# A two-layer hybrid attention encoder on one core: latent norms and latent outputs at other places in the order, part of the far shares on ScalarE, gains first in SP's queue

## The chip, the cores and the metric

The kernel runs on one core of one Trainium2 chip. Its engines are TensorE (PE, with PEld for the loading of weights), VectorE (DVE), ScalarE (ACT), GpSimd (POOL) and SyncE (SP, which here only issues transfers). The metric is the time of one execution on the device in microseconds (us); less is better.

## The reference

The input x is 512 positions by 1024 channels, float32. Two layers, each `x = x + concat(a, b) @ w_out`, and a last RMS norm. In a layer:

```
h = rms_norm(x, norm_g);  p = h @ w_in
c_q (384), c_kv (256), k_r (32), gate_a (512), dil_qkv (3 x 3 x 512), gate_b (512) = split(p)
a = mla_attention(c_q, c_kv, k_r) * silu(gate_a)
b = dilated_attention(dil_qkv) * silu(gate_b)
```

`mla_attention` norms the two latents c_q and c_kv (an RMS norm each), multiplies them up to queries, keys and values of 8 heads (64 plain and 32 rotary dimensions; one rotary key for all heads), and attends over all positions. `dilated_attention` has three groups of 8 heads of 64, with windows (128, 1), (512, 4) and (2048, 16) of (width, dilation), that is banded attention among neighbours and among every fourth and every sixteenth position; the outputs of the three groups are added with weights, the softmax over the groups' log-sums of exponentials, per position and head.

## The kernel before, in words

**Arithmetic.** Activations lie transposed, channels on partitions, in 8 tiles `h` of 128 x 512. Every operand of a large product is split into a high and a low part (`split`, L220: a cast on ScalarE, L221, and a subtraction on VectorE, L222), and a product is three matmuls (`triple`, L239: L241, L242, L243) of 512 columns. Weights come tile by tile from memory through SP's queue (`prefetch`, L189: L195), three tiles ahead of their use; ScalarE casts them (L198), and the low part is made by VectorE (L203) or, for most projections, by a negation on ScalarE (L200) and an accumulating load on GpSimd's queue (L201). A half chunk, that is 4 tiles of h against one weight tile, is 12 matmuls.

**The order.** All instructions are emitted by one planner, `Weave` (L76). It has a main line, TensorE's long products in the order of `forward_order` (L29), and side lines: `nline` (norms), `sline` (scores), `tline` (transposes of P and the products with V), `cline` (the combination of groups and the gated outputs). Each task is a generator that emits some instructions and yields an estimate of TensorE's time and a pause; the planner's clock is the sum of these estimates. A task has needs, (other task, lag): it may start when the clock has passed the end of the other by the lag. After each step of the main line the side lines are looked at, one task at a time in each; a line's next task waits for the one before it. When the main line is blocked, side steps are forced without regard to lags. What is emitted is then scheduled into the engines' queues by the framework, in which an instruction whose buffer isn't free can fall behind later ones. The planner's us are near TensorE's, but not the same.

**The parts that the change touches.**
- The start (L286 to L310): ScalarE's queue issues the first weight tile, the 26 columns of gains (`gn`, L289) and the second weight tile; SP's queue issues the 8 tiles of x (L298) and the other weight tiles. WARM matmuls on a zero tile (L296) run before the data are there. `take_x` (L270) multiplies x by the gains of the norm (L273, L274); the first products are L376.
- The latent norm (`latent_norm`, L388), task `lcq`: the squares of the query latent, added by GpSimd (L354), are transposed by TensorE (L256) and summed, 1/rms is worked out on VectorE in some 12 small instructions, and after a pause LN it is spread over partitions by TensorE (L236). `mla_rope`, task ("mur", 0), needs its end.
- The latent outputs (`mla_out`, L556, task "mo", one for each pair of heads): gate times output (`gated`, L430: L433), split into hl (L221, L222). They stand in `cline` between the combinations (`combine`, "do1", L813, and `combine_last`, "do", L835), in the order of the tasks that they belong to; the fourth "mo" comes after "do1" of pair 2. The output projection needs all four: `out_part` in layer 0, `out_rows` (L882) in layer 1.
- The far units (units 2 to 5 and 8 to 11: groups 1 and 2). `far_scores` (L727) makes scores, exponentials (L757) and, for group 2 in its second part, the groups' shares (`shares`, L795: L804 on ScalarE, L810 on VectorE the last), with which the 8 blocks of P are multiplied on GpSimd (L765). `far_out` (L768) transposes P (L449), splits it, and multiplies it with V in four steps (L785), each merged by ScalarE (L788) and VectorE (L789, L791). The lag between scores and transposes is LG2 = 16.5 for group 2 (units 4, 5, 10, 11) and LG = 6.0 for the others.

Of the kernel before, what the change touches and what calls it, by code (L numbers as in the profile page):

```python
# [11 lines left out]
ALU = mybir.AluOpType  # L12
# [10 lines left out]
AHEAD, RATE, LAG, CAP = 3, 451.1, 2.5, 34.9  # L23
STEP, LD0, WARM, LG2, LY = 2, 10.0, 11, 16.5, 5.0
LV = 3.0
LG, LP, LD, LM, LC, LN, LX, LF = 6.0, 0.25, 8.25, 2.0, 14.25, 5.75, 5.0, 0.25
SHUF = [i + 8 if i < 8 else i - 8 if i < 16 else i for i in range(32)]

def forward_order():  # L29
    return [('ckv',), ('v', 1, 0), ('cq', 2), ('cq', 0), ('cq', 1), ('dqk', 0, 0), ('dqk', 0, 1), ('nv', 0), ('mur', 0), ('ga', 0), ('dqk', 1, 0), ('kr',), ('dqk', 1, 1), ('nv', 1), ('muq', 0), ('muk', 0), ('mv', 0), ('muq', 1), ('dqk', 2, 1), ('muk', 1), ('dqk', 2, 0), ('muq', 2), ('dqk', 3, 1), ('muq', 3), ('dqk', 3, 0), ('dqk', 4, 1), ('mur', 1), ('v', 2, 0), ('muq', 4), ('dqk', 4, 0), ('dqk', 5, 0), ('muk', 2), ('ga', 1), ('muq', 5), ('dqk', 5, 1), ('mv', 1), ('dqk', 6, 0), ('nv', 2), ('gb', 0), ('muq', 6), ('dqk', 6, 1), ('muq', 7), ('nv', 3), ('dqk', 8, 0), ('gb', 1), ('muk', 3), ('v', 1, 1), ('ga', 2), ('dqk', 7, 0), ('dqk', 7, 1), ('dqk', 10, 0), ('dqk', 8, 1), ('dqk', 9, 0), ('dqk', 9, 1), ('v', 2, 1), ('dqk', 10, 1), ('ga', 3), ('dqk', 11, 0), ('dqk', 11, 1), ('gb', 2), ('gb', 3)]  # L30


def unit(u):

    return u % 6 // 2, 2 * (u // 6) + u % 2
# [102 lines left out]
def hybrid_encoder(ctx, tc, xT, wst, gains, fgain, tables, keytab, masks, out):  # L138
    nc = tc.nc
# [35 lines left out]
    gn = const.tile([128, 2 * NG], F32, name="gn")  # L175
# [102 lines left out]
    for l in range(DEPTH):  # L278
        L = Layer()
# [7 lines left out]
    load_w = lambda q, k: q.dma_start(raws[k], wst[k, :, 0:384])  # L287
    load_w(nc.scalar, 0)
    nc.scalar.dma_start(gn, gains)  # L289
    load_w(nc.scalar, 1)  # L290
    nc.scalar.activation(ones[:, 1:2], ones[:, 0:1], AF.Exp)
# [435 lines left out]
    def far_scores(L, u, part):  # L727
# [3 lines left out]
        g, p = unit(u)  # L731
# [3 lines left out]
        pt = t([128, S], F32, "p", 8)  # L735
# [3 lines left out]
        for j in range(2):  # L739
            b = 2 * part + j  # L740
# [19 lines left out]
        if g == 2 and part:  # L760
            shares(L, p)
            for b in range(4):
                for a in range(2):
                    pt = L.p["d", u, b // 2][:, 256 * (b % 2) + 128 * a:256 * (b % 2) + 128 * a + 128]
                    nc.gpsimd.tensor_scalar(pt, pt, L.share[p][:, b, 2, a:a + 1], 0.0, op0=ALU.mult, op1=ALU.add)  # L765
        yield 0.44, 0.5
# [164 lines left out]

    main, nline, sline, tline, cline = ([] for _ in range(5))
    for L in layers:
# [7 lines left out]
        task(nline, k("lckv"), later(k("ckv"), k("norm")), latent_norm, "ckv")  # L941
        task(nline, k("lcq"), later(*[k("cq", c) for c in range(3)], k("norm")), latent_norm, "cq")
        for o in ORDER:
# [43 lines left out]
        for _, (what, n), needs, scores, f in sorted(att, key=lambda x: x[0]):  # L987
            if scores:
                task(sline, k("s0", what, n), [(x, LM if what == "m" else LD0 if n == 0 else LD) for x in needs], scores, n, 0)
                task(sline, k("s", what, n), now(*before[0]), scores, n, 1)  # L990
                task(tline, k("o", what, n), [(k("s", what, n), LG2 if what == "d" and unit(n)[0] == 2 else LG)], f, n)
                before = [before[1], [("t", l, what, n)]]
            else:
                task(cline, k(what, n), needs, f, n)
        mla = [k("mo", p) for p in range(4)]
# [30 lines left out]

    Weave(RATE, CAP).run(main, [nline, sline, tline, cline])

# [114 lines left out]
```

## Time and profile before

| what | us |
|---|---|
| median of 3 runs | 930.44 (928.4 to 932.7) |
| the profiled execution, its own time | 929.99 |
| its span, first to last instruction | 928.2 |
| TensorE busy | 908.0 |
| VectorE, ScalarE, GpSimd busy | 692.4, 597.6, 313.2 |

In a row of the timeline stand start, duration, engine, line, operation, out<-in by the program's names, sizes, a count, and in brackets the idle time of the engine before it with what ended it. A "q" behind an engine's name is its sequencer, which issues transfers. Matmuls overlap, so their durations are longer than their spacing. The first products of layer 1 begin near 463 us.

### The profile page before, as it was taken

The page shows a single profiled execution, that of the slowest core. Times are in us where ns is not written, and L with a number is a line of the kernel's source. Part 1 is how long each engine was busy: PE and PEld are TensorE (multiplying, and loading weights), DVE is VectorE, ACT ScalarE, POOL GpSimd, SP SyncE. Part 2 cuts the span into 40 slices and gives each one's busy share as a digit, 9 for nine tenths or more (in the row PEclk, how much of TensorE's full clock was granted, in tenths as well). Part 3 has the DMA queues.
Part 4 walks back from the last instruction along what each step waited for, and adds up shares of the span by engine and source line. Part 5 has one row for each costly group of instructions (what it writes and reads, how often), then busy time and mean ns, then how long its engine had stood idle before and what let it go on. Part 6 is the DMA issues. An engine that isn't in the chain of part 4 may idle for free.

```text
span 928.2 us, 15855 instructions
## 1 busy us (share of the span) xinstructions
PE 908.0 (98%) x5175; PEld 773.4 (83%) x5175; DVE 692.4 (75%) x1733; ACT 597.6 (64%) x1449; POOL 313.2 (34%) x365
## 2 busy tenths in 40 slices
PE   9999999999999999999999999999999999999996
PEld 7978888988889889887897888889888888898785
DVE  6756787877868776688766679787878676767964
ACT  6546876667757766764445468756768586676533
POOL 0134253345542432233211343524464234224300
PEclk9999999999999999999999999999999999999998
DMA  8457453276554764664453653615667558367542
GB/s 271 121 124 146 97 123 69 65 163 148 122 124 93 148 125 107 137 155 132 166 169 95 146 121 82 126 40 134 138 126 158 129 101 167 78 142 138 147 125 91
DMA packets 86466, 118.14 MB, mean 127 GB/s; under 512 B 16944, under 2 KB 37232, under 8 KB 86384
## 3 DMA queue, kind: packets, MB, share of 16 engines
q1 hardware_dynamic: 66656, 81.59, 30.6%
q0 software_dynamic: 19296, 35.14, 24.0%
q8 instruction: 41, 0.67, 0.3%
q10 hardware_dynamic: 432, 0.41, 0.1%
q14 instruction: 41, 0.34, 0.1%
HBM read 112.74 MB, written 4.36 MB: 126 GB/s over the span
## 4 chain that ended last, share of the span: by engine, by line
PE 83%; DVE 8%; ACT 4%; issue 2%; DMA 1%; POOL 1%; ACTq 0%; DVEq 0%; POOLq 0%
PE bank L241 22%; PE bank L242 22%; PE bank L243 22%; PE bank L449 5%; PE bank L550 3%; PE bank L376 3%; PE bank L744 1%; PE bank L785 1%; PE bank L673 1%; DVE pt L222 1%; DVE whl L203 1%; ACT whl L198 1%; DMA p<-wst 1%; DMA wraw<-wst 1%; DVE tmp L630 1%
## 5 line engine op out<-in xcount | busy, mean ns | idle before, releaser
L241 PE MATMUL bank<-hl,whl 128*128 128x512 f32 x712 | 283.9, 399 | 2.2 <-ACT hl L221 1.3
L242 PE MATMUL bank<-hl,whl 128*128 128x512 f32 x712 | 278.3, 391 | 0.0
L243 PE MATMUL bank<-hl,whl 128*128 128x512 f32 x712 | 278.1, 391 | 0.0
L198 ACT CAST whl<-wraw 128x512 fp32r<-128x512 f32 (+3 forms) x243 | 143.8, 596 | 121.2 <-PE bank L243 80.2
L201 POOL DMA_DIRECT2D whl<-wst x134 | 117.9, 884 | 225.2 <-ACT whl L200 152.7
L243 PEld LDWEIGHTS bank<-hl,whl 128*128 128x128 f32 x712 | 133.6, 188 | 29.5 <-DMA whl<-wst 0.4
L241 PEld LDWEIGHTS bank<-hl,whl 128*128 128x128 f32 x712 | 133.7, 188 | 28.5 <-ACT hl L221 1.7
L242 PEld LDWEIGHTS bank<-hl,whl 128*128 128x128 f32 x712 | 134.0, 188 | 23.9 <-DVE hl L222 0.3
L241 PE MATMUL bank<-whl,hl 128*128 128x256 f32 (+2 forms) x328 | 99.6, 304 | 1.6 <-ACT hl L221 1.6
L243 PE MATMUL bank<-whl,hl 128*128 128x256 f32 (+2 forms) x328 | 97.9, 298 | 0.0
L242 PE MATMUL bank<-whl,hl 128*128 128x256 f32 (+2 forms) x328 | 97.7, 298 | 0.0
L628 POOL TENSOR_TENSOR tmp<-tmp,sd 128x512 f32<-128x512 f32 x48 | 63.2, 1316 | 91.9 <-DVE tmp L626 65.4
L203 DVE TENSOR_TENSOR whl<-wraw,whl 128x512 fp32r<-128x512 f32 (+3 forms) x109 | 76.6, 710 | 23.1 <-ACT whl L198 22.1
L222 DVE TENSOR_TENSOR pt<-bank,pt 128x512 fp32r<-128x512 f32 x128 | 83.6, 684 | 5.4 <-ACT pt L221 4.0
L200 ACT ACTIVATE whl<-wraw 128x512 fp32r<-128x512 f32 x134 | 85.0, 634 | 0.1
L221 ACT CAST pt<-bank 128x512 fp32r<-128x512 f32 x128 | 69.9, 588 | 10.7 <-PE bank L449 10.3
L530 POOL TENSOR_SCALAR p<-p,lc 128x512 f32<-128x512 f32 x64 | 48.8, 769 | 70.0 <-DVE lc L529 64.2
L449 PE MATMUL bank<-ident,p 128*128 128x128 f32 x512 | 67.7, 275 | 0.0
L241 PEld LDWEIGHTS bank<-whl,hl 128*128 128x128 f32 x328 | 62.3, 190 | 3.9 <-ACT hl L221 1.8
L243 PEld LDWEIGHTS bank<-whl,hl 128*128 128x128 f32 x328 | 62.3, 190 | 2.0 <-DVE hl L222 0.4
L242 PEld LDWEIGHTS bank<-whl,hl 128*128 128x128 f32 x328 | 62.4, 190 | 1.7
L449 PEld LDWEIGHTS bank<-ident,p 128*128 128x128 f32 x512 | 59.2, 142 | 5.4
(181 smaller groups left out, 1620.1 us busy)
## 6 DMA issues: line engine op xcount, KB each, us to landing
wraw<-wst SPq DMA_DIRECT2D x218, 256.0 KB, 3.1
whl<-wst POOLq DMA_DIRECT2D x134, 256.0 KB, 4.4
tmp<-shd SPq DMA_DIRECT2D x32, 128.0 KB, 4.3
xl<-xT SPq DMA_DIRECT2D x10, 256.0 KB, 2.9
wraw<-wst SPq DMA_DIRECT2D x16, 144.0 KB, 2.3
wraw<-wst SPq DMA_DIRECT2D x12, 192.0 KB, 2.6
x1d<-xl SPq DMA_DIRECT2D x8, 256.0 KB, 3.2
xl<-x1d SPq DMA_DIRECT2D x8, 256.0 KB, 3.2
```

The costliest lines, as they stand in the source:

```text
L198: nc.scalar.copy(hi, src)
L200: nc.scalar.mul(lo, src, -1.0)
L201: nc.gpsimd.dma_start(lo, wst[emitted[0], :, :c], accum_op=ALU.add)
L203: nc.vector.tensor_tensor(lo, src, F(hi), op=ALU.subtract)
L221: nc.scalar.copy(dst_hi, src)
L222: nc.vector.tensor_tensor(dst_lo, src, F(dst_hi), op=ALU.subtract)
L241: nc.tensor.matmul(a, w[:, 0], h[:, 0], start=first, stop=False)
L242: nc.tensor.matmul(a, w[:, 0], h[:, 1], start=False, stop=False)
L243: nc.tensor.matmul(a, w[:, 1], h[:, 0], start=False, stop=last)
L449: nc.tensor.transpose(b[:, 128 * i:128 * i + 128], x, ident)
L530: nc.gpsimd.tensor_scalar(pt, pt, l1, 0.0, op0=ALU.mult, op1=ALU.add)
L628: nc.gpsimd.tensor_tensor(u, u, L.sd, op=ALU.mult)
```

## The change

- The gains are the first transfer of SP's queue instead of the second of ScalarE's, and there are 9 warm matmuls instead of 11.
- In the main line ("mur", 0) comes after ("ga", 0) instead of before it, and their weight tiles change places with them.
- The lag from the chunks of c_q to the norm `lcq` is 5.0 instead of 2.5.
- The four "mo" tasks get a side line of their own, the last one, behind `cline`.
- In units 10 and 11 the four multiplies of P with a = 1 are done by ScalarE, the four with a = 0 stay on GpSimd. The lag to the transposes of these two units is 12.5 instead of 16.5.
- LO is defined and not used.

```
-STEP, LD0, WARM, LG2, LY = 2, 10.0, 11, 16.5, 5.0
-LV = 3.0
+STEP, LD0, WARM, LG2, LY = 2, 10.0, 9, 16.5, 5.0
+LV, LQ, LO, LGL = 3.0, 5.0, 4.0, 12.5
...
-    load_w(nc.scalar, 0)
-    nc.scalar.dma_start(gn, gains)
-    load_w(nc.scalar, 1)
+    nc.sync.dma_start(gn, gains)
+    for k in range(2):
+        load_w(nc.scalar, k)
...
-                    nc.gpsimd.tensor_scalar(pt, pt, L.share[p][:, b, 2, a:a + 1], 0.0, op0=ALU.mult, op1=ALU.add)
+                    share = L.share[p][:, b, 2, a:a + 1]
+                    if u >= 10 and a:
+                        nc.scalar.mul(pt, pt, share)
+                    else:
+                        nc.gpsimd.tensor_scalar(pt, pt, share, 0.0, op0=ALU.mult, op1=ALU.add)
...
-        task(nline, k("lcq"), later(*[k("cq", c) for c in range(3)], k("norm")), latent_norm, "cq")
+        task(nline, k("lcq"), [(k("cq", c), LQ) for c in range(3)] + later(k("norm")), latent_norm, "cq")
...
-                task(tline, k("o", what, n), [(k("s", what, n), LG2 if what == "d" and unit(n)[0] == 2 else LG)], f, n)
+                task(tline, k("o", what, n), [(k("s", what, n), LG if what == "m" or unit(n)[0] < 2 else LG2 if n < 10 else LGL)], f, n)
...
-                task(cline, k(what, n), needs, f, n)
+                task(gline if what == "mo" else cline, k(what, n), needs, f, n)
...
-    Weave(RATE, CAP).run(main, [nline, sline, tline, cline])
+    Weave(RATE, CAP).run(main, [nline, sline, tline, cline, gline])
```

`later` gives its tasks a lag of 2.5. `forward_order` differs only in the order `('nv', 0), ('ga', 0), ('mur', 0)`.

More of the change, by code (lines that the diff above doesn't have):

```diff
@@ L29, in forward_order @@
 def forward_order():
-    return [('ckv',), ('v', 1, 0), ('cq', 2), ('cq', 0), ('cq', 1), ('dqk', 0, 0), ('dqk', 0, 1), ('nv', 0), ('mur', 0), ('ga', 0), ('dqk', 1, 0), ('kr',), ('dqk', 1, 1), ('nv', 1), ('muq', 0), ('muk', 0), ('mv', 0), ('muq', 1), ('dqk', 2, 1), ('muk', 1), ('dqk', 2, 0), ('muq', 2), ('dqk', 3, 1), ('muq', 3), ('dqk', 3, 0), ('dqk', 4, 1), ('mur', 1), ('v', 2, 0), ('muq', 4), ('dqk', 4, 0), ('dqk', 5, 0), ('muk', 2), ('ga', 1), ('muq', 5), ('dqk', 5, 1), ('mv', 1), ('dqk', 6, 0), ('nv', 2), ('gb', 0), ('muq', 6), ('dqk', 6, 1), ('muq', 7), ('nv', 3), ('dqk', 8, 0), ('gb', 1), ('muk', 3), ('v', 1, 1), ('ga', 2), ('dqk', 7, 0), ('dqk', 7, 1), ('dqk', 10, 0), ('dqk', 8, 1), ('dqk', 9, 0), ('dqk', 9, 1), ('v', 2, 1), ('dqk', 10, 1), ('ga', 3), ('dqk', 11, 0), ('dqk', 11, 1), ('gb', 2), ('gb', 3)]
+    return [('ckv',), ('v', 1, 0), ('cq', 2), ('cq', 0), ('cq', 1), ('dqk', 0, 0), ('dqk', 0, 1), ('nv', 0), ('ga', 0), ('mur', 0), ('dqk', 1, 0), ('kr',), ('dqk', 1, 1), ('nv', 1), ('muq', 0), ('muk', 0), ('mv', 0), ('muq', 1), ('dqk', 2, 1), ('muk', 1), ('dqk', 2, 0), ('muq', 2), ('dqk', 3, 1), ('muq', 3), ('dqk', 3, 0), ('dqk', 4, 1), ('mur', 1), ('v', 2, 0), ('muq', 4), ('dqk', 4, 0), ('dqk', 5, 0), ('muk', 2), ('ga', 1), ('muq', 5), ('dqk', 5, 1), ('mv', 1), ('dqk', 6, 0), ('nv', 2), ('gb', 0), ('muq', 6), ('dqk', 6, 1), ('muq', 7), ('nv', 3), ('dqk', 8, 0), ('gb', 1), ('muk', 3), ('v', 1, 1), ('ga', 2), ('dqk', 7, 0), ('dqk', 7, 1), ('dqk', 10, 0), ('dqk', 8, 1), ('dqk', 9, 0), ('dqk', 9, 1), ('v', 2, 1), ('dqk', 10, 1), ('ga', 3), ('dqk', 11, 0), ('dqk', 11, 1), ('gb', 2), ('gb', 3)]
 def unit(u):
@@ L930, in out_sums @@
                 nc.sync.dma_start(rows[:, 512 * j + 256 * i:512 * j + 256 * i + 256], o[j][:, 256 * i:256 * i + 256])
-    main, nline, sline, tline, cline = ([] for _ in range(5))
+    main, nline, sline, tline, cline, gline = ([] for _ in range(6))
     for L in layers:
```

## The prediction

> **What bounds the kernel now.** I read the span and the engines' busy shares first, then who TensorE waited for, then the timeline at each of those places.
>
> ```profile
> core 0: 928.2 us, clock 0.996
> PE 908.0 (98%) x5175; PEld 773.4 (83%) x5175; DVE 692.4 (75%) x1733; ACT 597.6 (64%) x1449; POOL 313.2 (34%) x365
> ```
>
> The core is TensorE from end to end: 98% of the span, and no other engine above 75%. The change removes two matmuls of the start, whose result nobody uses, and no others. So it can win only where TensorE stands still, 20.2 us in all (928.2 less 908.0), with the wait for the first matmul and what follows the last one among them, where this change does nothing. Who it waits for inside the span is told by the waits of TensorE (engine, tile, line, releaser: total us, times, longest):
>
> ```profile
> PE bank L241 <- ACT hl L221: 2.9, 2, 1.6
> PE bank L256 <- POOL tmp L354: 1.8, 2, 0.9
> PE bank L785 <- DVE og L791: 0.7, 2, 0.4
> PE bank L376 <- ACT hl L273: 0.6, 2, 0.3
> ```
>
> Each appears twice: for the first three once per layer, and the fourth twice at the start. They are what the diff touches, 6.0 us together. The view understates them: a matmul is drawn 0.39 us long, but the next starts 0.23 us after it (422.18 and 422.41 below), so each stop costs about 0.16 us more than its idle time.
>
> **The start: gains first in SP's queue, two warm matmuls fewer.**
>
> ```profile
> 0.75 1.34 SPq L298 DMA_DIRECT2D og<-xT  x3
> 1.18 0.46 ACTq L289 DMA_DIRECT2D gn<-gains  x1
> 1.67 0.45 ACTq L287 DMA_DIRECT2D p<-wst  x1
> 1.49 4.51 PE L296 MATMUL bank<-q 128*128 128x512 f32 x11 [1.49 <-DVE q L293]
> 3.92 0.51 ACT L221 CAST hl<-p 128x384 fp32r<-128x384 f32 x1 [0.28 <-DMA p<-wst]
> 5.55 0.72 ACT L273 ACTIVATE hl<-og,gn 128x512 fp32r<-128x512 f32 x1 [1.11 <-DMA gn<-gains]
> 6.32 2.35 PE L376 MATMUL bank<-hl,hl 128*128 128x512 f32 x9 [0.32 <-ACT hl L273]
> 7.75 0.51 ACT L221 CAST hl<-p 128x384 fp32r<-128x384 f32 x1 [1.47 <-DMA p<-wst]
> 8.93 5.30 PE L376 MATMUL bank<-hl,hl 128*128 128x512 f32 x22 [0.26 <-ACT hl L273]
> ```
>
> The first product waits for L273, and L273 for the gains: 1.11 us, until 5.55. The gains go out at 0.75 instead of 1.18, and the second weight tile at 1.18 instead of 1.67, since the gains no longer stand before it on ScalarE. In return every one of SP's loads goes out about 0.45 us later. Without the wait for the gains, L273 can follow its cast L221, which ends at 4.43, and ends at about 5.15 if the first x tile is there; the nine warm matmuls end near 5.3 (11 take 4.51, the last two at the faster rate). The first product then starts near 5.4, 0.9 sooner. The second tile's products (8.93 now) hang on the weight tile that ScalarE casts at 7.75; it goes out 0.49 earlier and no longer shares its queue with the gains. Bounds for the whole start: 0, if the later x tiles give it back, to -1.4 (both stops gone, 0.32 + 0.26 with their overlap, and the tile landing 0.9 earlier). I take **-0.9**, the 5.55 row being the nearest.
>
> On that a page of the Trainium skill speaks against me: "DMA: Bandwidth & Descriptors", section "Issuing engines are not separate DMA queues", says all issuers share the same 16 engines, so another issuer only saves the issuing time. By it the sum would hold -0.4 here instead of -0.9; the trace has 4.4 us from the issue of these gains (1.18) to L273 (5.55), which suggests that more than issuing was in the way, but it does not separate the two.
>
> **Latent norm later, (mur, 0) after (ga, 0).**
>
> ```profile
> 51.14 1.27 POOL L354 TENSOR_TENSOR tmp<-tmp,tmp 128x512 f32<-128x512 f32 x1 [4.68 <-ACT tmp L350]
> 52.47 0.66 PE L256 MATMUL bank<-ident,tmp 128*128 128x128 f32 x4 [0.90 <-POOL tmp L354]
> ```
>
> The transposes of the query latent's squares reach TensorE while GpSimd still adds them. The lag from 2.5 to 5.0 puts them two half steps of the main line later (the side lines are looked at after each 6 matmuls): 12 x 0.23 = 2.7 us, against a stop of 0.90. The stop goes, in both layers: 2 x (0.90 + 0.16) = **-2.1**. The norm's second step and its end move on by as much; (mur, 0) stood exactly at that end and would have blocked the main line, but (ga, 0) now gives it 24 matmuls, 5.5 us, in between. (mur, 0)'s own consumers come five tasks later, its weight tile and the gate's change places in SP's queue, and the gate's rb is ready long before: 0, with bounds of -0.2 and +0.8 for work on VectorE that falls otherwise around the scores.
>
> **Latent outputs on a line of their own.** They cost the planner nothing; only the fourth one moves. It is due 2.5 planner us after gate (ga, 3), but stood behind the combine of pair 2, which waits for the other groups: it was released some 23 planner us later, right at the output products that read it.
>
> ```profile
> 417.19 0.22 ACT L804 ACTIVATE e<-e 128x24 f32<-128x24 f32 x1
> 418.55 1.28 POOL L832 TENSOR_TENSOR og<-og,og 128x512 f32<-128x512 f32 x1 [14.68 <-DVE ls L808]
> 419.17 1.21 DVE L433 SCALAR_TENSOR_TENSOR tmp<-mo,gate 128x512 f32<-128x512 f32 x1
> 420.31 0.17 DVE L810 TENSOR_TENSOR e<-e,ls 128x24 f32<-128x24 f32 x1
> 420.96 0.60 ACT L221 CAST hl<-tmp 128x512 fp32r<-128x512 f32 x1
> 421.61 0.73 PE L241 MATMUL bank<-hl,whl 128*128 128x512 f32 x2 [1.27 <-ACT hl L221]
> 422.18 0.39 PE L242 MATMUL bank<-hl,whl 128*128 128x512 f32 x1
> 422.41 0.40 PE L243 MATMUL bank<-hl,whl 128*128 128x512 f32 x1
> ```
>
> L433 (gate times output), L221 (cast), L241 (first product with it): the chain is complete, TensorE has nothing else. Layer 1 has the same one, with the last far unit behind it:
>
> ```profile
> 872.54 1.22 DVE L433 SCALAR_TENSOR_TENSOR tmp<-mo,gate 128x512 f32<-128x512 f32 x1
> 873.77 0.68 DVE L203 TENSOR_TENSOR whl<-wraw,whl 128x512 fp32r<-128x512 f32 x1
> 874.98 0.50 PE L241 MATMUL bank<-whl,hl 128*128 128x512 f32 x1 [1.61 <-ACT hl L221]
> 887.34 1.04 PE L449 MATMUL bank<-ident,p 128*128 128x128 f32 x8
> 894.37 0.87 PE L785 MATMUL bank<-pt,v 128*128 128x256 f32 x6
> 897.75 0.47 PE L785 MATMUL bank<-pt,v 128*128 128x256 f32 x2 [0.44 <-DVE og L791]
> 440.95 0.47 PE L785 MATMUL bank<-pt,v 128*128 128x256 f32 x2 [0.27 <-DVE og L791]
> ```
>
> Emitted 23 us earlier, the output is there long before: 1.27 + 1.61 + 2 x 0.16 = -3.2. What is late next: the low half of the weight, L203 at 873.77, which stood behind L433. Without it L203 can start at 872.8 and, if GpSimd's add of that moment holds it up as it did L433 (1.22 instead of 0.68 for L203, an equally large operation), ends near 873.9; the product that needs it would come at 873.7. That leaves 0.2: **-3.0**.
>
> **Last two far units.** The transposes of unit 10 are held by unit 9 on their line, so 12.5 for 16.5 changes nothing there. Unit 11's come 1.3 planner us earlier in layer 0, where the products with V are still forced in a block when the main line runs dry: the 0.27 at 440.95 stays. In layer 1 they come 3.7 earlier; their products then fall due one between each two main steps, before the line waits for them. The 0.44 at 897.75 goes: **-0.6**.
>
> Half of P's shares move to ScalarE:
>
> ```profile
> 396.98 3.59 POOL L765 TENSOR_SCALAR p<-p,e 128x128 f32<-128x128 f32 x8
> 400.15 0.62 ACT L200 ACTIVATE whl<-wraw 128x512 fp32r<-128x512 f32 x1
> 400.51 0.86 POOL L201 DMA_DIRECT2D whl<-wst  x1
> 403.81 0.62 ACT L221 CAST kst<-tmp 128x512 fp32r<-128x512 f32 x1 [3.03 <-DVE tmp L630]
> 411.34 0.40 ACT L757 ACTIVATE p<-p,st 128x128 f32<-128x128 f32 x1 [1.75 <-DVE st L753]
> whl<-wst POOLq DMA_DIRECT2D x134, 256.0 KB, 4.4
> ```
>
> GpSimd gives up 4 x 0.45 = 1.8 us per unit and ScalarE takes 4 x 0.40 = 1.6 (the exponentials of that shape). The shares are no longer late either way: the multiplies end at 400.57, and their transposes come among the exponentials of unit 11 (411.34). What counts is the queue behind them on ScalarE: at unit 10 also the cast of the moved latent output (0.60), together 2.2 us ahead of the weight casts. A weight tile is asked for three half chunks ahead, 3 x 12 x 0.23 = 8.3 us; cast, negation and accumulating load take 0.6 + 0.6 + 4.4 = 5.6. Of the slack of 2.7, 2.2 would be used, but GpSimd issues L201 up to 1.8 sooner, and ScalarE has 3.03 idle before 403.81. Bounds 0 and +2.4 over both layers; I take **+0.4**.
>
> **Sum:** -0.9 - 2.1 - 3.0 - 0.6 + 0.4 = -6.2. The profiled execution took 929.99 (928.2 and 1.8 around it), 0.45 below the median of 930.44, which makes no difference here: 929.99 - 6.2 = **923.8**. With the best and the worst bounds, -7.5 (1.4 + 2.3 + 3.2 + 0.6) and -2.5 (0 + 1.3 + 3.0 + 0.6 - 2.4): 922.5 to 927.5.
>
> **Rivals.** *The next one is late at once.* Removing a stop in a stretch where VectorE and ScalarE are back to back may only bring TensorE to the next weight or the next P. For it: L203 above is within 0.2 us of that. Against it: between 424 and 440 TensorE never stops. Were the latent outputs to bring nothing and the start 0, -2.1 - 0.6 remain, 927.3: a result within 0.5%.
>
> *Cold start.* The 11 warm matmuls run at 0.41 us, the real ones at 0.24 (4.51/11 and 5.30/22). If nine don't bring the full rate, the next ones run on slowly: for a stretch of some 3.3 us 3.3 / 0.41 = 8 more, at 0.17 each 1.4 lost, and with the -0.9 gone the time is 929.99 - 5.3 + 1.4 = 926.1. Such a stretch this trace does show, from 135.00 on:
>
> ```profile
> 135.00:138.30 3.30, 3.30 (x18) 2.75 (x17) 2.67 (x13) 2.44 (x10) 0.50 (x1) 0.50 0.79 140
> 590.00:593.30 3.30, 3.30 (x25) 2.79 (x25) 3.10 (x16) 2.76 (x11) 0.72 (x1) 1.00 0.69 133
> ```
>
> The same work in the two layers, once at a granted clock (third from the end) of 0.50 with 18 matmuls, once at 1.00 with 25. It costs some 7 x 0.23 = 1.6, and since it came in one of two like layers it may be there after the change or not; the sum leaves it in. The Trainium skill's "TensorE: Matmul & The Clock Gate", section "Part 1: The HAM clock gate", says the full rate needs about 3.4 us of sustained activity, in a window that runs freely; nine warm matmuls at 0.41 are an estimated 3.7, so by it the cut is narrow but enough, and it is why this rival has a chance of its own. That the clock fell at 135, with TensorE working most of the time before, is more than that section leads one to expect.
>
> *Slower: ScalarE waits for the shares.* ScalarE works in order. If the multiplies stand right behind the exponential of the shares (L804, ends 417.41), it stands still until VectorE has finished them (L810, ends 420.48): 3.1 us, then 1.6 of multiplies, before any weight cast. Past the slack of 2.7 every us reaches TensorE: 2.0 per unit, at four units 8.0, and with the stops of the latent outputs and the start coming back in other places (3.9), 929.99 - 2.1 - 0.6 + 8.0 = 935.3. Against it: the two operations are 3 us apart, and casts that are ready lie between.
>
> **Chances.** Forecast 0.62, next one late 0.22, cold start 0.08, ScalarE waits 0.06, other 0.02. About 0.5%, 4.65 us, is what a measurement of this kernel can tell from no change: under 925.8 is faster, over 935.1 slower. The forecast lies below with 0.57 and within with 0.05, the second and third within. The range goes from the best bound without the stretch of low clock (922.5 - 1.6 = 920.9) to the second case with one more of them (927.3 + 1.6 = 928.9), and leaves out what lies above. Faster 0.58, same 0.36, slower 0.06.
>
> **What would show it.** Right: TensorE's waits for L354 and for hl from L221 at the output products are gone in both layers; L433 of the fourth latent output stands near 398 and 851; the first product starts before 5.8; unit 11's L785 in layer 1 come in pairs with other products between. Wrong: a new stop of a microsecond or more near 400, 421, 853 or 873 with a weight or pt as releaser; the granted clock under 1 after 6 us; L765's transposes waiting for ScalarE.

## The result, and the profile after

The changed kernel is slower: 934.15 us in the median of 20 runs (930.11 to 941.10) against 929.60 of 20 runs of the kernel before (927.99 to 932.70). The ratio is 1.0051, with a 95% interval of 1.0038 to 1.0064, so some 4.7 us lost where 6.2 were to be gained. In what follows each ratio is turned into us with 929.6.

The execution that was profiled is the longest of the 20: 941.1 us, span 939.0. First the head of its page:

```profile
span 939.0 us, 15848 instructions
PE 913.3 (97%) x5173; PEld 778.6 (83%) x5173; DVE 691.5 (74%) x1733; ACT 601.4 (64%) x1465; POOL 303.7 (32%) x349
```

The span is 10.8 us longer. TensorE stands still for 25.7 us (939.0 less 913.3) instead of 20.2: 5.5 of the 10.8. The other 5.3 is busy time, although TensorE has two matmuls less to do. The timeline by windows shows why (start and end, length, busy time and count of PE, PEld, DVE, ACT and POOL, granted clock, DMA share, GB/s):

```profile
106.39:109.80 3.41, 3.41 (x9) 2.66 (x9) 2.53 (x10) 3.41 (x14) 0.00 (x0) 0.50 0.49 73
434.07:437.48 3.41, 3.41 (x11) 2.83 (x11) 3.03 (x6) 1.83 (x3) 1.09 (x1) 0.50 0.67 224
864.15:867.56 3.41, 3.41 (x9) 2.83 (x10) 2.37 (x5) 0.77 (x2) 0.00 (x0) 0.50 0.63 174
905.10:908.50 3.40, 3.40 (x11) 2.73 (x10) 2.07 (x3) 0.62 (x1) 0.00 (x0) 0.50 0.13 39
```

With the one from 901.70 to 905.10 that is five stretches at a granted clock of 0.50 where before has one (each trace has one more at its end, when little is left to do). Each costs at most half its length, 1.7 us.

They come and go between runs of one kernel. Each run's mean granted clock tells roughly how many it had: 0.989 in this execution, 0.994 in the median of the 20 runs of the changed kernel, and 0.998 in the median of the 29 runs of the kernel before that were taken beside the first experiments. A thousandth of the clock is up to 0.93 us. So, by this estimate, up to 4.7 of the 7 us by which this execution lies above its own median, and up to 3.7 of the 4.7 us that the median itself lost, are lost at the lower clock and not in the stops themselves. The two runs of the changed kernel at 0.997 took 930.11 and 931.34 us.

Who TensorE waited for (engine, tile, line, releaser: total, times, longest; the lines stand 4 lower than before from the diff's second part on, so L789 is the old L785, L795 the old L791):

```profile
PE bank L789 <- DVE og L795: 3.3, 1, 3.3
PE bank L243 <- DMA whl<-wst: 3.1, 2, 1.9
PE bank L449 <- DVE og L795: 3.1, 1, 3.1
PE bank L241 <- DVE st L680: 1.7, 2, 1.1
...
PE bank L242 <- DVE whl L203: 0.9, 1, 0.9
```

The waits for L354, for hl at the output products and for hl from L273, 5.3 us, are gone as forecast. In their place stand 10.4 us, of which 0.7 were there before: for weight tiles (L243, L242), and for the merge of a far unit (L449 and L789, which want a PSUM bank that L795 still reads). All of these lie around the last two far units, from 406 to 434 and from 864 to 902. The first of them, at unit 10 of the first layer:

```profile
396.63 1.28 ACT L767 ACTIVATE p<-p,e 128x128 f32<-128x128 f32 x4 [1.77 <-DVE e L814]
399.80 0.64 ACT L200 ACTIVATE whl<-wraw 128x512 fp32r<-128x512 f32 x1
400.74 0.89 POOL L201 DMA_DIRECT2D whl<-wst  x1 [1.93 <-ACT whl L200]
406.08 0.50 PE L243 MATMUL bank<-hl,whl 128*128 128x512 f32 x1 [1.21 <-DMA whl<-wst]
```

The four multiplies that ScalarE took over stand ahead of the casts and negations of weights. GpSimd, free sooner, now waits 1.93 us for L200 and issues L201 at 400.74, no sooner than before (400.51). TensorE would have used that tile 1.21 us earlier. And at the last unit of the second layer:

```profile
894.75 0.62 ACT L198 CAST hl<-wraw 128x512 fp32r<-128x512 f32 x1 [3.75 <-DMA wraw<-wst]
896.24 0.62 ACT L198 CAST whl<-wraw 128x512 fp32r<-128x512 f32 x1 [0.86 <-DMA wraw<-wst]
897.81 0.62 ACT L198 CAST whl<-wraw 128x512 fp32r<-128x512 f32 x1 [0.95 <-DMA wraw<-wst]
899.75 0.62 ACT L198 CAST whl<-wraw 128x512 fp32r<-128x512 f32 x1 [1.32 <-DMA wraw<-wst]
900.39 1.15 ACT L792 COPY tmp<-bank 64x256 f32<-64x256 f32 x3
901.90 0.87 DVE L795 TENSOR_TENSOR og<-bank,tmp 64x256 f32<-64x256 f32 x2
902.47 0.77 PE L789 MATMUL bank<-pt,v 128*128 128x256 f32 x2 [3.27 <-DVE og L795]
```

The products with V were done at 898.5, but the copies that empty their banks (L792) stand in ScalarE's queue behind casts that wait for raw weight tiles. ScalarE works there 0.62 us in every 1.5 to 1.9, and is still late.

### The profile page after: what moved, and what is told of

Read it like the earlier page. It is cut to its first block, busy times and chain, and to the rows that moved or that the text cites. A ratio compares the mean times of both kernels' runs of the same rounds, so it can differ in the third digit from the quotient of the medians.

```text
span 939.0 us, 15848 instructions
## 1 busy us (share of the span) xinstructions
PE 913.3 (97%) x5173; PEld 778.6 (83%) x5173; DVE 691.5 (74%) x1733; ACT 601.4 (64%) x1465; POOL 303.7 (32%) x349
## 4 chain that ended last, share of the span: by engine, by line
PE 79%; DVE 8%; ACT 5%; DMA 4%; issue 3%; POOL 0%; SPq 0%; DVEq 0%; ACTq 0%; POOLq 0%
PE bank L241 21%; PE bank L243 20%; PE bank L242 20%; PE bank L449 5%; PE bank L550 3%; PE bank L376 3%; DMA wraw<-wst 2%; PE bank L789 1%; PE bank L744 1%; DMA whl<-wst 1%; PE bank L673 1%; ACT whl L198 1%; DVE pt L222 1%; ACT p L757 1%; DVE whl L203 1%
## 5 line engine op out<-in xcount | busy, mean ns | idle before, releaser
L241 PE MATMUL bank<-hl,whl 128*128 128x512 f32 x712 | 284.7, 400 | 1.7 <-DVE st L680 1.7
L243 PE MATMUL bank<-hl,whl 128*128 128x512 f32 x712 | 279.3, 392 | 3.1 <-DMA whl<-wst 3.1
L242 PE MATMUL bank<-hl,whl 128*128 128x512 f32 x712 | 279.1, 392 | 0.0
L201 POOL DMA_DIRECT2D whl<-wst x134 | 118.2, 886 | 243.9 <-ACT whl L200 177.4
L243 PEld LDWEIGHTS bank<-hl,whl 128*128 128x128 f32 x712 | 134.3, 189 | 33.1 <-DMA whl<-wst 4.0
L241 PEld LDWEIGHTS bank<-hl,whl 128*128 128x128 f32 x712 | 134.4, 189 | 27.9 <-issue 1.6
L242 PEld LDWEIGHTS bank<-hl,whl 128*128 128x128 f32 x712 | 134.4, 189 | 23.6
L203 DVE TENSOR_TENSOR whl<-wraw,whl 128x512 fp32r<-128x512 f32 (+3 forms) x109 | 77.9, 720 | 30.2 <-ACT whl L198 29.2
L241 PE MATMUL bank<-whl,hl 128*128 128x256 f32 (+2 forms) x328 | 99.4, 303 | 0.0
L242 PE MATMUL bank<-whl,hl 128*128 128x256 f32 (+2 forms) x328 | 97.8, 298 | 0.9 <-DVE whl L203 0.9
L243 PE MATMUL bank<-whl,hl 128*128 128x256 f32 (+2 forms) x328 | 97.7, 298 | 0.0
L222 DVE TENSOR_TENSOR pt<-bank,pt 128x512 fp32r<-128x512 f32 x128 | 83.5, 683 | 5.5 <-ACT pt L221 4.1
L200 ACT ACTIVATE whl<-wraw 128x512 fp32r<-128x512 f32 x134 | 85.1, 635 | 0.1
L221 ACT CAST pt<-bank 128x512 fp32r<-128x512 f32 x128 | 69.8, 587 | 5.7 <-PE bank L449 5.3
L449 PE MATMUL bank<-ident,p 128*128 128x128 f32 x512 | 67.5, 274 | 3.1 <-DVE og L795 3.1
L449 PEld LDWEIGHTS bank<-ident,p 128*128 128x128 f32 x512 | 58.8, 141 | 8.7 <-issue 3.3
L242 PEld LDWEIGHTS bank<-whl,hl 128*128 128x128 f32 x328 | 62.4, 190 | 2.8 <-DVE whl L203 1.2
L241 PEld LDWEIGHTS bank<-whl,hl 128*128 128x128 f32 x328 | 62.3, 190 | 1.9
L243 PEld LDWEIGHTS bank<-whl,hl 128*128 128x128 f32 x328 | 62.4, 190 | 1.6
```

The lines of the kernel that those rows point to most:

```text
L200: nc.scalar.mul(lo, src, -1.0)
L201: nc.gpsimd.dma_start(lo, wst[emitted[0], :, :c], accum_op=ALU.add)
L203: nc.vector.tensor_tensor(lo, src, F(hi), op=ALU.subtract)
L221: nc.scalar.copy(dst_hi, src)
L222: nc.vector.tensor_tensor(dst_lo, src, F(dst_hi), op=ALU.subtract)
L241: nc.tensor.matmul(a, w[:, 0], h[:, 0], start=first, stop=False)
```

## The experiments

Eighteen kernels; the median, and the ratio to the kernel before run on the same chip. "Start and norm" is gains first, nine warm matmuls, the later latent norm and the swap.

| kernel | what it has | median | ratio (95%) |
|---|---|---|---|
| a1_pool | change, multiplies on GpSimd | 932.11 | 1.0032 (1.0016 to 1.0047) |
| a2_lag | change, transposes as late as before | 931.25 | 1.0028 (1.0014 to 1.0043) |
| a3_both | start and norm, own line | 931.17 | 1.0023 (1.0010 to 1.0036) |
| b1_line | own line alone | 933.63 | 1.0051 (1.0036 to 1.0066) |
| b2_head | start and norm alone | 928.06 | 0.9990 (0.9980 to 1.0000) |
| a5_noline | change without own line | 930.82 | 1.0017 (1.0006 to 1.0028) |
| d_fill | own line, 24 idle matmuls more | 941.95 | 1.0134 (1.0118 to 1.0150) |
| d_mid | own line, fourth output later | 932.09 | 1.0040 (1.0024 to 1.0055) |
| e_wraw5 | own line, five raw buffers | 931.29 | 1.0020 (1.0006 to 1.0034) |
| f_wraw5 | before, five raw buffers | 928.31 | 0.9989 (0.9979 to 0.9998) |
| e_copy | own line, PSUM copies on VectorE | 936.00 | 1.0078 (1.0064 to 1.0093) |
| g_mid_wraw5 | start and norm, own line later, five buffers | 926.06 | 0.9968 (0.9956 to 0.9980) |
| g_lag | the same, transposes sooner | 927.06 | 0.9976 (0.9967 to 0.9985) |
| h_all | the same, with multiplies on ScalarE too | 928.16 | 0.9984 (0.9971 to 0.9996) |
| g_sub | g_mid_wraw5, one low half by GpSimd | 923.20 | 0.9934 (0.9916 to 0.9953) |
| e_mid_wraw5 | own line later, five buffers | 928.90 | 0.9996 (0.9985 to 1.0007) |
| e_sub | the same, one low half by GpSimd | 927.04 | 0.9967 (0.9956 to 0.9978) |
| f_sub | before, five buffers, one low half by GpSimd | 929.52 | 0.9998 (0.9989 to 1.0007) |

**Which part costs?** My first theory (A and B) was the trace's two pictures above: the multiplies and the sooner transposes cost, the rest gains. The rival (T2) was that TensorE, wherever it is made earlier, only meets the next late thing. The edits, against the changed kernel for the first two and against before for the last:

```
a1_pool:  if u >= 10 and a:   ->   if u >= 12 and a:
a2_lag:   LGL 12.5 -> 16.5
a3_both:  both
b1_line:  task(cline, k(what, n), ...)  ->  task(gline if what == "mo" else cline, k(what, n), ...)
```

> After the change, but all of P's multiplies back on GpSimd. Theory A (the four multiplies on ScalarE stand ahead of the cast and negation of the next weight tile, L198 and L200, so the tile lands late: L243 waits 1.38 us at 406.08 and 2.08 us at 864.12, and a stretch of 3.4 us at half clock follows, about 1.5 us more): both stops go and one or two of the half-clock stretches with them, 934.2 - 3.5 - 1.5 to 3 = 928 to 929.5. Rival T2 (TensorE has merely become earlier than its weights, whoever multiplies): 934 within 1, and both stops of L243 stay.

> After the change, but unit 11's transposes due as late as before (16.5). Theory B (sooner, they find no PSUM bank, because ScalarE's copy of the merge of unit 10, L792, stands behind weight casts; TensorE takes its instructions in order and stands still at L449 or L789, 3.2 us at 433.96 and 3.4 us at 902.47, plus about 1.5 us of half clock each): 934.2 - 6 to 9 = 925 to 928. Rival T2 (the merges of the last units are late whatever the lag): 933 to 935, with a stop of about 3 us on DVE og in both layers.

> After the change, with both undone: what is left is the start, the later latent norm with the swap, and the own line of the fourth latent output. If theories A and B are all of the loss: the prediction's sum without its last two terms, 929.6 - 0.9 - 2.1 - 3.0 = 923.6, perhaps 0.5 more for the later full clock of the start. Rival T2: 930 to 934, with new stops of a microsecond or more near 406, 434, 864 and 902.

> The kernel before, with only the latent outputs on a line of their own. By the prediction's term: 3.0 us faster, 926.6, with no stop of L241 on hl at 421.6 and 875.0. If the own line by itself makes the weight tiles late (T2): 929 to 931, with a stop on whl in place of the one on hl.

The first theory fell. a1_pool and a2_lag each came out between their two forecasts. In a1_pool the stops of L243 shrank from 3.1 to 0.5 us, as theory A has it, but L242 stood still for 2.3 behind L203, where the changed kernel has 0.9. With both parts undone (a3_both) the kernel is still 0.23% slower than before, 2.1 us, and the own line alone costs 0.51%, 4.7 us: as much as the whole change. (Its six runs have a median clock of 0.996, so by the same estimate up to 1.9 of these 4.7 us are the clock's.) The multiplies alone add 0.05% to a3_both and the transposes alone 0.09%, neither of which the intervals tell from nothing; the two together add 0.28%, 2.6 us. The waits of TensorE with the own line alone:

```profile
PE bank L785 <- DVE og L791: 3.3, 2, 2.8
PE bank L242 <- DVE whl L203: 2.3, 1, 2.3
...
PE bank L785 <- DVE pt L222: 1.4, 1, 1.4
PE bank L243 <- DMA whl<-wst: 1.3, 2, 1.1
```

The two stops for hl (2.9) are gone, and these four rows hold 8.3 us, of which 0.7 were there before. TensorE's instructions stand almost in the same order as before (in the first layer one pair of L785 lies six matmuls later), so the cause is in what the other engines do, and when. In ScalarE's queue in the second layer the copies (L788) are late again, without the multiplies and with the transposes at their old place. The cast that waited for a load lies 6 us ahead of them here; the two directly ahead waited for TensorE and for VectorE:

```profile
892.05 0.62 ACT L198 CAST hl<-wraw 128x512 fp32r<-128x512 f32 x1 [2.48 <-DMA wraw<-wst]
892.58 0.58 ACT L221 CAST pt<-bank 128x512 fp32r<-128x512 f32 x1
...
896.27 0.62 ACT L198 CAST whl<-wraw 128x512 fp32r<-128x512 f32 x1 [2.08 <-PE bank L785]
...
897.64 0.62 ACT L198 CAST whl<-wraw 128x512 fp32r<-128x512 f32 x1 [0.74 <-DVE whl L203]
898.28 1.15 ACT L788 COPY tmp<-bank 64x256 f32<-64x256 f32 x3
...
900.36 0.47 PE L785 MATMUL bank<-pt,v 128*128 128x256 f32 x2 [2.80 <-DVE og L791]
```

**The gaining parts by themselves, and two theories of the own line.** H2: TensorE comes early to what other engines do late in any case. H1: the fourth output, emitted 23 planner us sooner, gets in the way of other work there. (In the trace of b1_line its L433 starts at 388.9 instead of 419.2, and at 845.1 instead of 872.5.)

```
b2_head:    before, with gains first, WARM 9, LQ 5.0, and ("ga", 0) ahead of ("mur", 0)
a5_noline:  task(cline, k(what, n), ...) again
d_fill:     b1_line, and ahead of the first output product of each layer
            for _ in range(12): nc.tensor.matmul(a, ms[0][:, 0, 0:128], ms[0][:, 0], start=True, stop=True)
d_mid:      b1_line, with mo 3 due 12.0 after gate and head instead of LAG (2.5)
```

> The kernel before with only the start (gains first, nine warm matmuls), the later latent norm and the swap of (mur, 0) with (ga, 0). By the prediction's terms: 929.6 - 0.9 - 2.1 = 926.6. By the runs so far, if the parts add: own line alone 933.6, own line with these edits 931.2, so these edits bring 2.4: 927.2. If TensorE's lead is always lost again in the last units (T2): 929 to 930, with longer stops at 421 and 875.

> After the change, without the own line of the latent outputs (the fourth waits behind the combine of pair 2 again); multiplies on ScalarE and the sooner transposes stay. If the own line is the cause of most of the loss and the parts add: 934.2 - 4.0 = 930. If the multiplies and the sooner transposes cost by themselves whatever the line does: 927.2 + 3 = 930 as well, but with stops of L243 on the weight near 406 and 864, and on DVE og near 434 and 902; if these come only because TensorE is early there (T2), 927 to 928 without them.

> Own line alone, and 12 matmuls of 512 columns whose result nobody uses, 2.7 us of TensorE's time, ahead of the first output product of each layer (5.4 us in all). H2 (after the old stop is gone TensorE only comes early to weights, P and PSUM banks that the other engines are late with): they hide in those stops, 933.6 plus at most 1. H1 (the fourth output, emitted 23 us earlier, pushes back work of VectorE and ScalarE near 395 and 851, and that is the loss): 937 to 939.

> Own line alone, but the fourth latent output due 12 planner us after its gate and head instead of 2.5: its L433 comes some 6 us later, after the merge of unit 9 and the low half of its P, and still long before the output products. H1: the stops of L243 on the weight at 404.65 (1.28) and 859.86 (0.37) go, with part of the stops after them, 930 to 931.5. H2: 933 to 934, the stops at 431, 438, 441, 876 and 900 as they are.

Start and norm alone bring 0.10%, 0.9 us, at the edge of what the interval tells from nothing, instead of 3.0: all the stops that they were to remove are gone, but others have grown (L241 behind L680: 1.2 instead of 0.9, and L243 on a weight tile):

```profile
PE bank L241 <- DVE st L680: 1.2, 1, 1.2
...
PE bank L243 <- DMA whl<-wst: 0.6, 1, 0.6
```

Without the own line the changed kernel is still 0.17% slower, and 0.27% slower than b2_head: the multiplies and the transposes cost 2.5 us whether the line is there or not.

H2 in its plain form is refuted. The 24 matmuls, 5.4 us, did not hide in those stops but cost 0.83%, 7.7 us. Not all of that is their own time: the five runs of d_fill have a median clock of 0.992, against 0.996 with the own line alone, which is up to 3.7 us, and the two profiled executions, at 0.997 and 0.998, lie only 6.0 us apart (939.32 and 933.28). The stop for L203 went; that for og stayed, and that for P's low half (pt, L222) doubled:

```profile
PE bank L785 <- DVE pt L222: 2.9, 1, 2.9
PE bank L785 <- DVE og L791: 2.7, 1, 2.7
```

That the other engines go by TensorE as well may add to it, which no run here shows by itself. Here is the group of weight casts in the kernel before (busy time, mean ns, idle time ahead of them and who ended it):

```profile
L198 ACT CAST whl<-wraw 128x512 fp32r<-128x512 f32 (+3 forms) x243 | 143.8, 596 | 121.2 <-PE bank L243 80.2 <-issue 20.6 <-DMA wraw<-wst 12.1
```

Of 121.2 us that ScalarE idles ahead of them, 80.2 end when TensorE gives a tile free. A TensorE that comes later would be served later. H1 may have a part: with a later due time the stop at 404.65 is gone, but only 0.11%, 1.0 us, comes back, which the intervals do not tell from nothing.

**What is ScalarE's queue worth?** H3: the casts that wait for `DMA wraw<-wst` are what stops TensorE.

```
e_wraw5, f_wraw5:  raw = t([128, 512], F32, "wraw", 3)  ->  ... 5     (on b1_line, on before)
e_copy:            b1_line, L788 of units 10 and 11: nc.scalar.copy -> nc.vector.tensor_copy
g_mid_wraw5:       a3_both, with d_mid's due time and five buffers
```

> Own line alone, with five buffers for raw weight tiles instead of three, so that SP can ask for a tile without waiting for VectorE and ScalarE to be done with the third last. Theory H3 (the stops of the output stretch come because casts L198 that wait for `DMA wraw<-wst` stand in ScalarE's queue ahead of the copies L788 and of P's casts L221, which TensorE needs): the stops at 431.7, 437.8, 440.9 and 900.4 (6.2 us together) mostly go, 928 to 929. If VectorE's own queue is what is late (it is busy 9.4 of 10 us from 860 to 880): 933 to 934.

> The kernel before with five buffers for raw weight tiles, the comparison for the run above. Before has no stop of over 0.6 us that these buffers could touch, so 929 to 930 under both theories; if it is faster by more than 1 us, the gain of the run above is not the own line's.

> Own line alone, with the PSUM copies L788 of units 10 and 11 on VectorE instead of ScalarE: eight copies of about 0.4 us per layer leave ScalarE's queue, where they stand behind casts that wait for DMA. H3: the stops on DVE og at 431.7, 440.9 and 900.4 (4.6 us) go, that on pt at 437.8 stays, 929 to 930. If VectorE is the late one: 934 to 936, since it gets 3 us more work per layer.

> The start, later latent norm, swap and own line of the change, without multiplies on ScalarE and sooner transposes, with the fourth latent output due at 12 and five buffers for raw weight tiles. If H3 holds and the parts add: 929.4 - 1.1 (start and norm) - 3.0 (own line's term, now kept) + 0.5 = 926. If VectorE is the late one: 930.

Eleven weight tiles of the output products are cast into tiles named hl. Here is their group in the kernel before, with the own line alone, and with five buffers too:

```profile
L198 ACT CAST hl<-wraw 128x512 fp32r<-128x512 f32 x11 | 6.7, 619 | 3.3 <-DMA wraw<-wst 3.3
```

```profile
L198 ACT CAST hl<-wraw 128x512 fp32r<-128x512 f32 x11 | 6.8, 618 | 10.3 <-DMA wraw<-wst 10.3
```

```profile
L198 ACT CAST hl<-wraw 128x512 fp32r<-128x512 f32 x11 | 6.7, 618 | 2.9 <-DMA wraw<-wst 2.7
```

The own line had made their wait for loads three times as long, and five buffers undo that. No wait for og is left on TensorE's list either, though a new one stands there (L449 behind L753, 1.8 us). So H3 names a real wait, but not all of the loss: the own line still costs 0.31% (1.0020 against 0.9989), 2.9 us instead of 4.7. To take the copies out of ScalarE's queue by giving them to VectorE makes it worse, 936.0, as forecast if VectorE is the late one. With five buffers and the later due time together the change's gaining parts at last gain, 926.06. That 926 had been forecast is luck: it counted -3.0 for the own line and -1.1 for start and norm, where the runs below put +0.7 (inside the intervals) and -2.6. What then stands in TensorE's way in the second layer is one L203:

```profile
869.21 1.26 POOL L836 TENSOR_TENSOR og<-og,og 128x512 f32<-128x512 f32 x1 [16.65 <-DVE el L810]
869.73 0.17 DVE L812 TENSOR_REDUCE ls<-el 128x8 f32<-128x24 f32 x1
869.82 1.21 DVE L203 TENSOR_TENSOR whl<-wraw,whl 128x512 fp32r<-128x512 f32 x1
...
871.08 0.50 PE L242 MATMUL bank<-whl,hl 128*128 128x512 f32 x1 [1.55 <-DVE whl L203]
```

The weight's high half was cast from 866.21; its low half waits 3 us in VectorE's queue and then takes 1.21 instead of 0.68, since GpSimd adds at the same time. GpSimd had stood idle 16.65 us until then.

**VectorE's queue, and the own line's true term.**

```
g_sub, e_sub, f_sub:  (nc.gpsimd if (l, key) == (DEPTH - 1, ("wo", 3, 0)) else nc.vector).tensor_tensor(lo, src, F(hi), op=ALU.subtract)
                      on g_mid_wraw5, on e_mid_wraw5, on f_wraw5
g_lag:                g_mid_wraw5, LGL 16.5 -> 12.5
h_all:                g_lag, and if u >= 10 and a: nc.scalar.mul(pt, pt, share)
e_mid_wraw5:          d_mid, five buffers
```

> The run with the fourth output due at 12 and five raw buffers (926.06), but the low half of one weight tile (the fourth of the last layer's output products) by GpSimd, which has nothing to do from 862 to 869, instead of by VectorE. If VectorE's queue is what is late there (its L203 stands behind the last unit's scores and the combine and takes 1.21 us beside GpSimd's add; L242 waits 1.72 us at 871.1): that stop goes, 924.3 to 925. If TensorE meets the next late thing at once: 926, with as long a stop within 10 us behind it.

> The same run (926.06), but unit 11's transposes due at 12.5 again instead of 16.5. Theory B (the sooner transposes stop TensorE because the copies that free their PSUM banks stand in ScalarE behind casts that wait for `DMA wraw<-wst`): with five raw buffers those casts hardly wait, so the cost of the sooner transposes goes, 925.5 to 926.5. If the merges are late for another reason: a stop of 1 to 3 us on DVE og near 430 and 895 again, 927.5 to 929.

> The whole change, with two things taken out of its way: the fourth latent output due at 12 instead of 2.5, and five raw buffers instead of three. If the multiplies on ScalarE and the sooner transposes cost only through the casts that wait for raw weights: 926 to 927. If the multiplies cost through the weight cast and negation behind them (L198, L200, stops of L243 of 1.4 and 2.1 us in the changed kernel): 928 to 930, with those two stops.

> The kernel before with the own line, the fourth latent output due at 12, and five raw buffers: nothing of the start or the norm. The term of the own line with both obstacles out of its way, against before with five raw buffers (928.3). The prediction's term: -3.0, 925.3. If the parts add: 926.06 + 1.1 = 927.2, so -1.1.

> The kernel before with the own line, the fourth output due at 12, five raw buffers and the one low half by GpSimd: the own line with all three obstacles out of its way, and nothing of the start or the norm. If the stop of L242 on VectorE's L203 at 875.0 (1.72) is what ate the gain there: 928.9 - 1.7 to 2.9 = 926 to 927.2. If the gain in the run with the start and norm came from those: 928.5.

> The comparison for it: before with five raw buffers and the one low half by GpSimd, the fourth output on its old line. There L241 waits 1.70 us for the cast of that output (872.7), not for the low half: 928 to 928.5 if nothing else hangs on VectorE's queue, 927 if the cast comes sooner by the 0.7 us that VectorE saves. Own line's term is then the difference to the run above: -1 to -2, where the prediction had -3.0.

One subtraction moved to the idle engine is worth 0.34%, 3.2 us, more than the stop that it removes (1.55). It now runs there long before it is needed, and L242 no longer waits:

```profile
866.60 1.29 POOL L203 TENSOR_TENSOR whl<-wraw,whl 128x512 fp32r<-128x512 f32 x1 [14.35 <-ACT whl L198]
```

g_sub, at 923.20 us, is the fastest kernel of the study, 0.66% under before, and has neither the multiplies on ScalarE nor the sooner transposes. On g_mid_wraw5 those add 0.08% each, 0.7 us, inside the intervals; the two together add 0.16%, 1.5 us, and the intervals still overlap. With five buffers the transposes no longer wait for a bank, but TensorE, so much earlier, waits for the cast of the last far output instead (L241 at 435.09 behind L221 in g_lag: 2.1 us, where 0.7 was), and in the traces of g_lag and h_all a stretch at half clock follows there.

The own line, step by step: 0.51% alone (b1_line), 0.31% with five buffers (e_wraw5 to f_wraw5), 0.07% with the later due time as well (e_mid_wraw5 to f_wraw5, inside the intervals), and with the low half by GpSimd -0.31% (e_sub to f_sub) or, since that edit by itself adds 0.09% to f_wraw5, also inside the intervals, -0.22% against f_wraw5. So it gains 2.0 to 2.9 us once three things are out of its way. That f_sub did not gain was not expected; with the subtraction gone from VectorE the old stop there grew, from 1.53 in f_wraw5 to 2.62. TensorE came to it sooner and the cast did not: L241 starts at 872.66 in f_wraw5 and at 872.67 here.

```profile
870.26 1.18 DVE L433 SCALAR_TENSOR_TENSOR tmp<-mo,gate 128x512 f32<-128x512 f32 x1
...
872.67 0.79 PE L241 MATMUL bank<-whl,hl 128*128 128x512 f32 x1 [2.62 <-ACT hl L221]
```

L433 takes its 1.18 beside GpSimd's add, as it did in before. Only with the own line as well, which has L433 done long ago, does the freed time reach TensorE: on five buffers, neither of the two edits shows a gain without the other.

## Why the prediction was wrong, step by step

**What bounds the kernel** was right: TensorE, and only its stops are to be won. But the four rows of stops were read as a list of prices that add. The hl row's two stops stand where VectorE (the fifth column) is busy over 9 us of 10, as the windows of the kernel before show:

```profile
415.00:425.00 10.00, 8.73 (x41) 6.75 (x40) 9.44 (x27) 5.58 (x17) 5.63 (x5) 1.00 0.22 62
...
870.00:880.00 10.00, 8.39 (x42) 6.59 (x41) 9.84 (x22) 5.82 (x14) 7.17 (x9) 1.00 0.47 138
```

There a stop of TensorE is where it falls in step with the others; taken out at one place, it comes back at the next.

**Latent outputs on a line of their own, -3.0: the step that failed.** It measured +4.7 (b1_line). The working asked what is late next and answered "That leaves 0.2", from one row, L203 in the second layer. That row was the right one and its price wrong by a factor of ten: 2.3 us in b1_line. And it was one of four; the weight tile at 404, the PSUM banks of the merges and P's cast were not looked for, since "between 424 and 440 TensorE never stops". That an engine never stops says nothing about how much slack it has. The half-clock stretches, too, were put at nothing: the range allowed for one more or less by chance, not for their following the new stops, which in the median may be up to 3.7 us of the whole loss. That the fourth output was late before, and that moving it can gain, was right: with the three obstacles gone the term is -2.0 to -2.9.

**The start and the latent norm, -0.9 and -2.1.** All their stops went, as forecast: the first product starts at 5.50, and L354 is off TensorE's list in both layers. The start's size was right as well: up to 9.85 us TensorE begins 15 to 20 products in the ten traces with the new start, 18.1 in the mean, and 9 to 16 in the ten with the old, 14.2 in the mean; 3.9 x 0.23 is 0.9 us. Alone the two bring -0.9 (b2_head), with new stops at 103 to 106 and at 856, so there the norm's part came to about nothing. On kernels with five buffers they bring -2.6 (g_mid_wraw5 to e_mid_wraw5) and -3.1 (g_sub to e_sub): the sum of the two terms, 3.0, was the right size for a kernel that can use it.

**Last two far units, -0.6.** It comes out at +0.7 in the best surroundings (g_lag), inside the intervals, and the stop at 897.75 became one of 3.3 us at 902.47. That is not the lag's alone: a2_lag, with the old lag, has 2.17 us there, a3_both 0.54. The step counted when the products become due, but not that they need PSUM banks, which ScalarE empties behind its waiting casts.

**Half of P's shares, +0.4.** The slack argument held in kind: the four multiplies reach the next weight tile, and 0.7 us of cost (h_all to g_lag, inside the intervals) lies within its bounds of 0 and +2.4. It missed that GpSimd's saved 1.8 us are worth nothing at unit 10, as L201 waits for ScalarE's L200 anyway, and its slack counted 4.4 us, the median, for a load that took 5.5 there in the kernel before already. What it could not see from one part is that transposes and multiplies together cost 2.5 to 2.6 us with three raw buffers.

**Rivals.** *The next one is late at once* named the mechanism, but with zero gain as its worst, 927.3; that moving a wait can cost more than the wait was not considered. *Slower* had the sign and the engine, ScalarE. It does wait for the shares, as the line's own view of the changed kernel says (releaser: total, times),

```profile
  DVE e L814: 5.3, 4
```

but 1.3 us a unit and not 3.1, and a nearly equal wait in a2_lag (4.8) costs next to nothing. That its 935.3 lies near the measured 934.15 is luck. More hangs on the raw weights that ScalarE waits for: five buffers take 1.8 of the own line's 4.7 us away. *Cold start* had some truth, but not through the cut from eleven to nine: after the same start the first products run at different rates in two runs (first the changed kernel, then a3_both):

```profile
5.50 4.35 PE L376 MATMUL bank<-hl,hl 128*128 128x512 f32 x14
```

```profile
5.50 4.34 PE L376 MATMUL bank<-hl,hl 128*128 128x512 f32 x18
```

Four matmuls fewer in the same time, some 0.9 us. But eleven leave the full rate to chance just as well: it sets in between 5.1 and 7.1 us in the ten traces with eleven, and between 5.1 and 7.4 in the ten with nine.

On the gains' issuer, the Trainium skill ("DMA: Bandwidth & Descriptors", section "Issuing engines are not separate DMA queues") gave only the issuing time. L273, which waited for the gains, starts at 4.51 to 4.77 us in the ten traces with the gains first and at 5.01 to 5.55 in the ten others, 0.6 sooner in the mean, against 0.4 for the issuing. The first product came 0.82 us sooner (6.32 to 5.50), but 5.50 is where the ninth warm matmul ends, so how much of that is the gains' and how much the shorter warm-up's is not separated.

What stays open: how the cost of the multiplies and transposes divides, since each alone is inside the intervals, and how much of each median is exactly the clock's, since a run's mean clock gives only an upper bound.

## What to carry to other kernels

A stop on the bounding engine is worth its length only if everything behind it is early by at least as much. Before pricing it, list for the next 30 us what each instruction of that engine needs, who makes it, and what stands ahead of that in its maker's in-order queue, waits for DMA first. Where several stops belong to one chain, one edit may lose what two or three together gain; test them in pairs before throwing one away. And look at the granted clock of every run before a median is put down to the stops alone.

## What the hardware showed that was not expected

Away from their ends, 11 of the 20 traces show stretches at a granted clock of 0.50, 16 in all, of 3.41 us each, once two in a row. All begin in a stop or within 2 us of its end, but the length of a stop alone does not decide: in the changed kernel they follow stops of 3.06 and 1.9 us, before has one at 134.9 behind two of under 0.6, and the stop of 2.80 us that ends at 900.36 in b1_line has none behind it.

They keep a beat. In the changed kernel they begin at 106.39, 434.07, 864.15 and 901.70, which lie 96, 126 and 11 times 3.413 us apart, and in every trace with more than one, the one at the end included, they lie whole beats apart. What seems to count is how long TensorE stands still within one beat. Seven beats have more than 1.9 us of that, and each has a stretch behind it; of five with 1.8 to 1.9, two have; of the many below, seven. In b1_line a beat ends at 899.40, eight beats before the stretch at its end (926.71), so the 2.80 us there fall into two beats, 1.84 and 0.96.

The Trainium skill's "TensorE: Matmul & The Clock Gate", section "HAM oscillation — how this bites in real kernels", sums its rule up as no idle gap on TensorE of over some 3.4 us; here the clock fell behind gaps of 0.5 to 3.3 us, so the shorter stops of a kernel that is 97% busy must be reckoned with too, at up to 1.7 us each.

The low half's 1.21 us beside GpSimd's add fits a lock held by one at a time: L836 ends at 870.47, L203 started at 869.82 and ends at 871.03, 0.56 after that, not far from the 0.68 that it takes alone. So says the Trainium skill's "SBUF — State Buffer", section "SBUF: two separate sides", of an operation of VectorE with two SBUF inputs against one of GpSimd that reads SBUF. The same operation on GpSimd itself took 1.29 us.
